# Modulation products in fixed runs of two row blocks, and latent attention with one 96-row tile per head

## The chip, the cores and the metric

The kernel runs on one core of a Trainium2 chip. The time is device microseconds from the start to the end of one execution; less is better. Engines are named PE (TensorE), DVE (VectorE), ACT (ScalarE), POOL (GpSimd) and SP (the engine that issues nearly all DMAs here). All matrices are float32; the dense ones are multiplied in three passes of a rounded type (fp32r, a high and a low part), the small ones plainly in float32, which shows as two records for each matmul.

## What is computed

Two transformer-like blocks on 256 tokens of width 1024: a first block of two layers with modulation by a condition vector (`DEPTH = 2`), and a second of one layer with three mixing branches. Two parts matter here.

The modulation vectors of a layer are a product of two vectors (the condition and its counterpart for the context) with a 1024 x 9216 matrix:

```python
mod_x = (jax.nn.silu(c) @ w_ada[l] + b_ada[l])[:, None, :]
mod_c = jax.nn.silu(c_ctx) @ w_ada[l] + b_ada[l]
```

Latent attention in the second block has 8 heads; each query and key is 64 plain and 32 rotated numbers, the rotated part of the key being shared by all heads:

```python
logits = (jnp.einsum('bhqd,bhkd->bhqk', q_nope[:, :, q0:q1], k_nope[:, :, :q1])
          + jnp.einsum('bhqd,bkd->bhqk', q_rope[:, :, q0:q1], k_rope[:, :q1]))
probs = _masked_softmax(logits * scale, mask)
return jnp.einsum('bhqk,bhkd->bhqd', probs.astype(v.dtype), v[:, :, :q1])
```

The 256 queries go in two blocks of 128; the second sees 256 keys, the first 128.

## The kernel before

**How it is put together.** The Python code doesn't issue instructions. It records them in program order in a `Plan`, with an estimated cost each (`cost`), and `schedule` then lays them out by a list schedule: on each engine, whenever it is free, the earliest recorded operation that is ready and whose buffers find room. `emit` issues the operations in that order, all from line 739, so every row of the profile has that line, and rows are told apart by their forms. Each engine executes its own list in order. A group of matmuls recorded under `with nc.run():` is one operation of the plan: its matmuls stay together, and it has one cost.

**Memory.** SBUF work tiles live in 22 pages of 2048 words per partition (45,056 in all). An operation out of program order gets new buffers only if what in-order execution will need, plus a reserve, still fits (`safe`, `can`); the reserve is the last argument of `schedule` in `build`, `dict(m=4096, s=64)`, and `3000` is how many operations ahead it may go. Some tiles have a cap of their own (`tag`, `bufs`): weights `wraw` 3 landing slots, their high and low halves 4 each, modulation weights `araw` 3 pages.

**Modulation.** `ada_steps(l, g)` makes the steps of group g of layer l: 2048 columns of the matrix in groups 0 to 3, 1024 in group 4. One step per block of 128 rows (eight of them) loads 128 x 2048 words (1 MB) and multiplies it in four products of 512 columns, each with a stationary operand of 32 columns (two vectors, padded), so that product j goes to the array's column strip j and to partitions 32 j of one PSUM bank; half-width groups use two strips. The eight steps add up in the bank, and a last step `fin` turns the result by four products per group into columns. Group 0 of layer 0 is executed at the start, with eight buffers of its own. All others are put in a list (`self.fill`), and one step is taken from it after each gate-and-up step (22) and each down step (16) of a feed-forward block: groups 1 to 4 of layer 0 (36 steps) in the first block, the five groups of layer 1 (45 steps) in the second, and what is left right after the block.

**Latent attention.** `mla_diff` projects queries (`w2_uq`: four 128-column blocks of plain parts, two heads each, then two blocks of rotated parts, four heads each) and keys. `qn`, `kn` hold the plain parts, head h in rows 64 (h % 2) on; `qr` the rotated query parts, head h in rows 32 (h % 4) on; `kr` the rotated key part four times over. `rope32` rotates a 128-row tile. Then for each pair of heads (b) and each head (s): scores of two query blocks, each as a 64-row product and a 32-row product that add up in PSUM; mask, softmax; three transposes; three products with the values, whose outputs go to rows 64 s on. `transposed` and the softmax also serve the branch behind it (differential attention).

The stages by time in the profile: first modulation group to 35 us; feed-forward to 455; mixing to 690; feed-forward to 1115 and, in layer 1, to 1497; mixing to 1648; feed-forward to 1870; then the second block, with the recurrent branch to 2055, latent attention to 2105, differential attention and merging to 2262, feed-forward to the end.

Of the kernel before, what the change touches and what calls it, by code (L numbers as in the profile page):

```python
# [18 lines left out]
P = 128  # L19
# [725 lines left out]
class Build:  # L745
# [134 lines left out]
    def ada_steps(self, l, g):  # L880

        nc = self.nc
        n = min(2048, 9 * D - 2048 * g)
        nj = n // 512
        st = {}

        early = l == 0 and g == 0

        def load(k):
            def f():  # L890
                if k == 0:
                    st["ps"] = self.aux_ps("ada")
                raw = self.sb.tile([P, 2048], F32, name="araw", tag="araw0" if early else "araw",
                                   bufs=8 if early else 3)
                nc.sync.dma_start(raw[:, :n], self.a["w_ada"][l, k, :, 2048 * g:2048 * g + n])
                for j in range(nj):
                    nc.tensor.matmul(st["ps"][32 * j:32 * j + 32, :], self.cs[:, k, :],
                                     raw[:, 512 * j:512 * j + 512], start=(k == 0), stop=(k == KB - 1),
                                     skip_group_check=True, tile_position=(0, 32 * j))
            return f  # L900

        def fin():
            np_ = 32 * nj
            t = self.t("adat", [512])
            nc.vector.tensor_copy(t[:np_], st["ps"][:np_])
            pt = self.aux_ps("adaT")
            for b in range(4):
                nc.tensor.matmul(pt[:, 8 * b:8 * b + 8], t[:np_, 128 * b:128 * b + 128], self.rsel[:np_],
                                 start=True, stop=True)
            view = pt[:, :32].rearrange("p (b j r) -> p b j r", b=4, j=4)[:, :, :nj]  # L910
            dst = self.mod[l][:, 16 * g:16 * g + 4 * nj, :].rearrange("p (j b) r -> p b j r", b=4)
            bia = self.b_ada[l][:, 16 * g:16 * g + 4 * nj, :].rearrange("p (j b) r -> p b j r", b=4)
            nc.vector.tensor_tensor(dst, view, bia, op=OP.add)
            for m in range(2 * g, 2 * g + nj // 2):
                w = self.mod[l][:, KB * m:KB * m + KB, :]
                if m % 3 == 1:
                    i = m // 3
                    nc.vector.scalar_tensor_tensor(
                        self.G[l][i], w, 1.0, self.gains[:, l, i, :, None].to_broadcast([P, KB, 2]),
                        op0=OP.add, op1=OP.mult)  # L920
                elif m in (2, 8):
                    nc.vector.tensor_scalar(self.hg[l][m // 8], w, 0.5, None, op0=OP.mult)
        return [load(k) for k in range(KB)] + [fin]


# [950 lines left out]
    def rope32(self, dst, src):  # L1876
        nc = self.nc
        pr = self.aux_ps("rot")
        nc.tensor.matmul(pr[:, :S], self.perm2, src, start=True, stop=True)
        t1, t2 = self.t256("rp1"), self.t256("rp2")  # L1880
        nc.vector.tensor_tensor(t1, src, self.rope2[:, 0], op=OP.mult)
        nc.vector.tensor_tensor(t2, pr[:, :S], self.rope2[:, 1], op=OP.mult)
        nc.vector.tensor_tensor(dst, t1, t2, op=OP.add)

    def mla_diff(self, u):
# [38 lines left out]
        kr, qr = self.s2("kr", (S,)), self.s2("qr")  # L1924
        self.rope32(kr, x[3])
        qn, kn = ([self.s2(f"{n}{i}") for i in range(2)] for n in ("qn", "kn"))
        w = self.wtile(a["w2_uq"])
        for i in range(3):
# [3 lines left out]
            if i < 2:  # L1932
                nc.scalar.copy(qn[i].rearrange("p a b -> p (a b)"), ps)
            else:
                t = self.t512("qrt")
                nc.scalar.copy(t, ps)
                for j in range(2):
                    self.rope32(qr[:, j], t[:, S * j:S * j + S])
        w = self.wtile(a["w2_ukv"])
        for i in range(2):  # L1940
# [3 lines left out]
            nc.scalar.copy(kn[i].rearrange("p a b -> p (a b)"), ps)  # L1944
# [25 lines left out]
        def transposed(pr):  # L1970
            pt = self.aux_ps("PT2")
            for i in range(3):
                nc.tensor.transpose(pt[:, P * i:P * i + P], pr[:, P * i:P * i + P], self.ident)
# [4 lines left out]
        for b in range(4):  # L1978
            yp = self.aux_ps("y")
            for s in range(2):  # L1980
                h = 2 * b + s
                hs = slice(64 * s, 64 * s + 64)
                rr = slice(32 * (h % 4), 32 * (h % 4) + 32)
                ps = self.aux_ps("Sml")
                for qt, (c0, c1) in enumerate(span):
                    qs = slice(P * qt, P * qt + P)
                    N = c1 - c0
                    nc.tensor.matmul(ps[:, c0:c1], qn[b // 2][hs, b % 2, qs], kn[b // 2][hs, b % 2, :N],
                                     start=True, stop=False)
                    nc.tensor.matmul(ps[:, c0:c1], qr[rr, h // 4, qs], kr[rr, :N], start=False, stop=True,  # L1990
                                     tile_position=(32 * (h % 4), 0))
# [7 lines left out]
                pts = transposed(pr)  # L1999
# [84 lines left out]
def build(tc, aps, out):  # L2084
# [6 lines left out]
    order = plan.schedule(N_PAGES, N_SMALL, W_SLOTS, 3000, dict(m=4096, s=64))  # L2091
# [27 lines left out]
```

## Time and profile before

| | before |
|---|---|
| median of 3 runs (lowest, highest) | 2465.49 us (2462.23, 2465.62) |
| the profiled execution: its time | 2465.52 us |
| its span, first to last instruction | 2463.7 us |
| mean granted TensorE clock | 0.986 |
| TensorE matmul busy | 2419.1 us, 14630 records |
| VectorE busy | 1342.4 us |
| ScalarE busy | 971.2 us |
| GpSimd busy | 46.5 us |
| HBM read | 325.00 MB, 132 GB/s over the span |

Busy time is the union of an engine's instructions; an engine that is busy may still work on a few rows or columns of its array, and successive matmuls overlap in the records by 0.07 to 0.16 us, so sums of durations exceed the time. A clock of 1.00 is 2.4 GHz, 0.50 is 1.2 GHz. In rows by form, `128*32 128x512` is a matmul with 128 rows and 32 columns of stationary operand and 512 columns moving; `page` and `bank` are SBUF and PSUM, `small` the page of small tiles. A window counts every instruction that overlaps it.

### The profile page before, as it was taken

Reading aid. Unit: us, or ns where it says so; the run is one execution under the profiler, and the core shown is the slowest. Engines: PE = TensorE matmul, PEld = TensorE weight load, DVE = VectorE, ACT = ScalarE, POOL = GpSimd, SP = SyncE. Lnnn points to the kernel's source line nnn. Section 1 sums busy time; section 2 is a strip of 40 time slices with the busy share of each in tenths; the row PEclk is TensorE's granted clock in tenths of the full one; section 3 lists DMA queues with packets and bytes.
Section 4 is the critical chain, followed back from the end, with each engine's and each line's share of the span. In section 5 each row is a group of like instructions: output and inputs, shape, how many; then the busy total and the mean of one; then the engine's idle time right before and its main releaser. Section 6 shows DMA issues by size and latency. Waiting matters only on the chain. (4 is left out here: it accounts for less than half of the span.)

```text
span 2463.7 us, 35734 instructions
## 1 busy us (share of the span) xinstructions
PE 2419.1 (98%) x14630; PEld 2036.2 (83%) x14630; DVE 1342.4 (54%) x2533; ACT 971.2 (39%) x1748; POOL 46.5 (2%) x62
## 2 busy tenths in 40 slices
PE   7999999999999999999999999999999999999998
PEld 5777776978787677778878889889999897999998
DVE  4323332585753389335323347866567665657874
ACT  3222222476642122223212235755456122556653
POOL 0000000000000000000000000000000000000000
PEclk8999999999999999999999999999999997999999
DMA  7526523212234454343224223135554011354543
GB/s 312 205 103 240 197 87 127 95 44 87 85 137 161 146 190 180 131 156 139 91 71 137 75 100 103 61 113 178 196 171 164 22 52 35 104 190 169 190 168 123
DMA packets 55043, 328.35 MB, mean 133 GB/s; under 512 B 7134, under 2 KB 10206, under 8 KB 24799
## 3 DMA queue, kind: packets, MB, share of 16 engines
q1 hardware_dynamic: 54878, 326.07, 37.1%
q8 instruction: 114, 1.87, 0.3%
q14 instruction: 51, 0.41, 0.1%
HBM read 325.00 MB, written 1.05 MB: 132 GB/s over the span
## 5 line engine op out<-in xcount | busy, mean ns | idle before, releaser
L739 PE MATMUL bank<-page,page 128*128 128x256 f32 (+8 forms) x13152 | 2296.3, 346 | 29.0 <-DMA page<-in_w_ada_dram 13.2
L739 PEld LDWEIGHTS bank<-page,page 128*128 128x128 f32 (+3 forms) x13152 | 1876.1, 186 | 373.8 <-issue 95.1
L739 ACT CAST page<-w 128x1024 fp32r<-128x1024 f32 (+2 forms) x511 | 489.1, 961 | 1067.6 <-PE bank L739 1027.6
L739 DVE TENSOR_TENSOR page<-w,page 128x1024 fp32r<-128x1024 f32 (+2 forms) x511 | 567.8, 1113 | 591.5 <-ACT page L739 457.8
L739 DVE TENSOR_TENSOR page<-page,bank 128x512 f32<-128x512 f32 (+2 forms) x170 | 94.2, 570 | 245.3 <-PE bank L739 244.1
L739 PE MATMUL bank<-page 128*128 128x256 f32 (+5 forms) x650 | 167.0, 325 | 1.9 <-DVE page L739 1.3
L739 DVE SCALAR_TENSOR_TENSOR page<-bank,small,page 128x256 f32<-128x256 f32 (+2 forms) x240 | 111.5, 484 | 103.8 <-PE bank L739 100.2
L739 DVE TENSOR_TENSOR page<-page,page 128x256 fp32r<-128x256 f32 (+3 forms) x271 | 128.6, 490 | 12.1 <-ACT page L739 11.5
L739 ACT ACTIVATE page<-bank,small 128x256 f32<-128x256 f32 (+2 forms) x216 | 115.1, 546 | 37.3 <-DVE small L739 24.8
L739 PEld LDWEIGHTS bank<-page 128*128 128x128 f32 (+2 forms) x650 | 109.8, 188 | 15.9 <-issue 4.2
L739 ACT CAST page<-page 128x256 fp32r<-128x256 f32 (+1 forms) x167 | 78.2, 481 | 97.0 <-DVE page L739 86.5
L739 ACT COPY page<-bank 128x512 f32<-128x512 f32 (+2 forms) x163 | 77.6, 511 | 96.5 <-PE bank L739 91.1
L739 PEld LDWEIGHTS bank<-small,page 128*128 128x128 f32 (+1 forms) x760 | 93.2, 167 | 25.0 <-issue 8.7
L739 PE MATMUL bank<-small,page 128*128 128x128 f32 (+4 forms) x760 | 108.8, 269 | 4.1 <-ACT page L739 2.8
L739 ACT ACTIVATE page<-bank 128x512 f32<-128x512 f32 (+3 forms) x168 | 84.2, 508 | 61.3 <-PE bank L739 57.8
L739 ACT ACTIVATE page<-page 128x256 f32<-128x256 f32 (+3 forms) x180 | 78.0, 446 | 67.0 <-DVE page L739 60.0
L739 DVE TENSOR_TENSOR page<-bank,page 128x256 f32<-128x256 f32 (+2 forms) x123 | 57.5, 489 | 55.4 <-PE bank L739 29.6
L739 DVE TENSOR_REDUCE small<-bank 128x1 f32<-128x512 f32 (+3 forms) x132 | 67.5, 527 | 4.3 <-PE bank L739 4.0
L739 POOL TENSOR_TENSOR small<-small 128x2 f32<-128x2 f32 (+2 forms) x32 | 34.4, 1078 | 1874.3 <-DVE small L739 1382.8
L739 ACT ACTIVATE page<-page,small 128x256 fp32r<-128x256 f32 (+1 forms) x124 | 56.7, 507 | 30.5 <-DVE page L739 30.0
L739 DVE COPY_PREDICATED page<-page,small 128x384 f32<-128x384 uint32 x124 | 64.9, 590 | 1.0
L739 DVE TENSOR_SCALAR page<-page,small 128x256 f32<-128x256 f32 (+2 forms) x136 | 53.6, 408 | 2.2 <-ACT page L739 1.1
(46 smaller groups left out, 383.2 us busy)
## 6 DMA issues: line engine op xcount, KB each, us to landing
w<-in_gu_dram SPq DMA_DIRECT2D x88, 1024.0 KB, 5.0
page<-in_w_ada_dram SPq DMA_DIRECT2D x64, 1024.0 KB, 4.9
w<-in_dn_dram SPq DMA_DIRECT2D x64, 704.0 KB, 4.1
w<-in_w_up_dram SPq DMA_DIRECT2D x22, 1024.0 KB, 4.8
w<-in_w_qk_dram SPq DMA_DIRECT2D x12, 1024.0 KB, 4.8
w<-in_w_gate_dram SPq DMA_DIRECT2D x12, 1024.0 KB, 4.9
w<-in_w_dn_dram SPq DMA_DIRECT2D x16, 704.0 KB, 4.0
page<-in_w_ada_dram SPq DMA_DIRECT2D x16, 512.0 KB, 3.5
```

The costliest lines, as they stand in the source:

```text
L739: getattr(getattr(self.real, eng), m_)(*a_, **k_)
```

## The change

Modulation: a step now takes two row blocks (`nk = 2`, but one for the early group): two loads, then all their products as one run with a cost of 215 ns a product plus 200. In a half-width group the second block goes to strips 2 and 3, so that these sum separately, and `fin` adds both halves by two products per column block. The buffers `araw` become 4.

Latent attention: `qh`, `kh` hold each head's 64 plain rows and, below them, its 32 rotated rows, in one tile of 96 rows. ScalarE copies each head's 64 rows out of PSUM by itself (`heads`, four copies of 64 x 256 for one of 128 x 512); `rope32` writes the rotated rows head by head; GpSimd copies the rotated key part to all heads. Scores are one product of 96 rows per query block. The transposes are a run; the value products of a pair of heads come together in one run, the two heads by turns.

The reserve of the plan goes from 4096 to 6144 words.

```diff
@@ ada_steps
-        def load(k):
+        nk = 1 if early else 2
+        def load(k0):
             def f():
...
-                raw = self.sb.tile([P, 2048], F32, name="araw", tag="araw0" if early else "araw",
-                                   bufs=8 if early else 3)
-                nc.sync.dma_start(raw[:, :n], self.a["w_ada"][l, k, :, 2048 * g:2048 * g + n])
-                for j in range(nj):
-                    nc.tensor.matmul(st["ps"][32 * j:32 * j + 32, :], self.cs[:, k, :],
-                                     raw[:, 512 * j:512 * j + 512], start=(k == 0), stop=(k == KB - 1),
-                                     skip_group_check=True, tile_position=(0, 32 * j))
+                raws = []
+                for k in range(k0, k0 + nk):
+                    raw = self.sb.tile([P, 2048], F32, name="araw", tag="araw0" if early else "araw",
+                                       bufs=8 if early else 4)
+                    nc.sync.dma_start(raw[:, :n], self.a["w_ada"][l, k, :, 2048 * g:2048 * g + n])
+                    raws.append(raw)
+                with nc.run(cost=nk * nj * 215.0 + 200.0):
+                    for i, raw in enumerate(raws):
+                        k = k0 + i
+                        for j in range(nj):
+                            c = 32 * (j if nj == 4 else j + nj * i)
+                            nc.tensor.matmul(st["ps"][c:c + 32, :], self.cs[:, k, :], raw[:, 512 * j:512 * j + 512],
+                                             start=k < (1 if nj == 4 else 2), stop=k >= KB - (1 if nj == 4 else 2),
+                                             skip_group_check=True, tile_position=(0, c))
...
         def fin():
...
+            m = 2 * nj
             for b in range(4):
-                nc.tensor.matmul(pt[:, 8 * b:8 * b + 8], t[:np_, 128 * b:128 * b + 128], self.rsel[:np_],
-                                 start=True, stop=True)
+                for c in range(0, 8, m):
+                    nc.tensor.matmul(pt[:, 8 * b:8 * b + m], t[:, 128 * b:128 * b + 128], self.rsel[:, c:c + m],
+                                     start=c == 0, stop=c + m == 8)
...
-        return [load(k) for k in range(KB)] + [fin]
+        return [load(k) for k in range(0, KB, nk)] + [fin]
@@ rope32
-        nc.vector.tensor_tensor(dst, t1, t2, op=OP.add)
+        for dst, rows in dsts:
+            nc.vector.tensor_tensor(dst, t1[rows], t2[rows], op=OP.add)
@@ mla_diff
-        qn, kn = ([self.s2(f"{n}{i}") for i in range(2)] for n in ("qn", "kn"))
+        qh, kh = ([self.s2(f"{n}{i}", (4, S)) for i in range(2)] for n in ("qh", "kh"))
+        for i in range(2):
+            nc.gpsimd.tensor_copy(kh[i][64:96], kr[64:96, None, :].to_broadcast([32, 4, S]))
+
+        def heads(dst, i, ps):
+            for j in range(2):
+                for s in range(2):
+                    nc.scalar.copy(dst[i][:64, 2 * j + s], ps[64 * s:64 * s + 64, S * j:S * j + S])
...
-                nc.scalar.copy(qn[i].rearrange("p a b -> p (a b)"), ps)
+                heads(qh, i, ps)
...
-                    self.rope32(qr[:, j], t[:, S * j:S * j + S])
+                    self.rope32([(qh[j][64:96, h], slice(32 * h, 32 * h + 32)) for h in range(4)],
+                                t[:, S * j:S * j + S])
...
-            nc.scalar.copy(kn[i].rearrange("p a b -> p (a b)"), ps)
+            heads(kh, i, ps)
...
         def transposed(pr):
-            for i in range(3):
-                nc.tensor.transpose(pt[:, P * i:P * i + P], pr[:, P * i:P * i + P], self.ident)
+            with nc.run():
+                for i in range(3):
+                    nc.tensor.transpose(pt[:, P * i:P * i + P], pr[:, P * i:P * i + P], self.ident)
...
-                    nc.tensor.matmul(ps[:, c0:c1], qn[b // 2][hs, b % 2, qs], kn[b // 2][hs, b % 2, :N],
-                                     start=True, stop=False)
-                    nc.tensor.matmul(ps[:, c0:c1], qr[rr, h // 4, qs], kr[rr, :N], start=False, stop=True,
-                                     tile_position=(32 * (h % 4), 0))
+                    nc.tensor.matmul(ps[:, c0:c1], qh[h // 4][:96, h % 4, P * qt:P * qt + P],
+                                     kh[h // 4][:96, h % 4, :c1 - c0], start=True, stop=True)
...
+            with nc.run(cost=3 * 215.0):
                 for qt in range(2):
                     for kb in range(qt + 1):
                         c0 = (qt + kb) * P
-                        nc.tensor.matmul(yp[hs, P * qt:P * qt + P], vm[kb][:, 64 * h:64 * h + 64], pts[:, c0:c0 + P],
-                                         start=(kb == 0), stop=(kb == qt), skip_group_check=True)
+                        for s in range(2):
+                            h, hs = 2 * b + s, slice(64 * s, 64 * s + 64)
+                            nc.tensor.matmul(yp[hs, P * qt:P * qt + P], vm[kb][:, 64 * h:64 * h + 64],
+                                             ptss[s][:, c0:c0 + P], start=(kb == 0), stop=(kb == qt),
+                                             skip_group_check=True)
@@ build
-    order = plan.schedule(N_PAGES, N_SMALL, W_SLOTS, 3000, dict(m=4096, s=64))
+    order = plan.schedule(N_PAGES, N_SMALL, W_SLOTS, 3000, dict(m=6144, s=64))
```

## Rows read from the trace of the kernel before

**Rows 1.** The page: busy time, share of the span and instructions of each engine.

```profile
PE 2419.1 (98%) x14630; PEld 2036.2 (83%) x14630; DVE 1342.4 (54%) x2533; ACT 971.2 (39%) x1748; POOL 46.5 (2%) x62
```

**Rows 2.** The page's forty slices: TensorE's granted clock, DMA rate.

```profile
PEclk8999999999999999999999999999999997999999
...
GB/s 312 205 103 240 197 87 127 95 44 87 85 137 161 146 190 180 131 156 139 91 71 137 75 100 103 61 113 178 196 171 164 22 52 35 104 190 169 190 168 123
```

**Rows 3.** Waits of TensorE: us in total, times, longest.

```profile
PE bank L739 <- DMA page<-in_w_ada_dram: 13.2, 5, 6.6
```

**Rows 4.** Groups by form, 35-1200 us: busy us, mean ns, idle.

```profile
L739 PE MATMUL bank<-page,page 128*32 128x512 f32 x512 | 103.5, 604 | 0.0
```

**Rows 5.** By form: stretches at 49.1, 77.9, 693.6 us in turn.

```profile
L739 PE MATMUL bank<-page,page 128*32 128x512 f32 x2 | 1.0, 604 | 0.0
...
L739 PE MATMUL bank<-page,page 128*32 128x512 f32 x8 | 1.1, 604 | 0.0
...
L739 PE MATMUL bank<-page,page 128*32 128x512 f32 x10 | 1.9, 602 | 0.0
```

**Rows 6.** By form: 172-178 us with a load, 132-138 us without.

```profile
L739 PE MATMUL bank<-page,page 128*128 128x512 f32 x23 | 5.7, 395 | 0.0
...
L739 PE MATMUL bank<-page,page 128*128 128x512 f32 x28 | 6.5, 389 | 0.0
```

**Rows 7.** By form, 2055.2-2093.2 us: score products of latent attention.

```profile
L739 PE MATMUL bank<-page,page 32*128 32x256 f32 x16 | 9.2, 673 | 0.0
L739 PE MATMUL bank<-page,page 64*128 64x256 f32 x16 | 8.7, 641 | 0.0
L739 PE MATMUL bank<-page,page 64*128 64x128 f32 x16 | 5.7, 454 | 0.0
L739 PE MATMUL bank<-page,page 32*128 32x128 f32 x16 | 5.7, 452 | 0.0
```

**Rows 8.** By form: 32-row pairs, 2056.5-2057.9 us; last, 2073.1-2075.2 us.

```profile
L739 PE MATMUL bank<-page,page 32*128 32x256 f32 x2 | 0.7, 426 | 0.0
L739 PE MATMUL bank<-page,page 32*128 32x128 f32 x2 | 0.5, 321 | 0.0
...
L739 PE MATMUL bank<-page,page 32*128 32x256 f32 x2 | 1.2, 708 | 0.0
```

**Rows 9.** Stretches: length; busy PE, PEld, DVE, ACT, POOL; TensorE clock; DMA.

```profile
2060.00:2070.00 10.00, 10.00 (x30) 5.75 (x28) 6.55 (x26) 2.13 (x9) 1.05 (x1) 0.60 0.21 89
...
2090.00:2100.00 10.00, 10.00 (x51) 7.64 (x50) 3.09 (x14) 3.92 (x15) 0.00 (x0) 0.69 0.00 0
```

**Rows 10.** By form, 35-1200 us: products that end a modulation group.

```profile
L739 PE MATMUL bank<-small,page 128*128 128x8 f32 x56 | 6.8, 242 | 0.0
```

**Rows 11.** By form, full clock: 256-column products at 2049.9-2050.9 us.

```profile
L739 PE MATMUL bank<-page,page 128*128 128x256 f32 x5 | 1.2, 376 | 0.0
```

**Rows 12.** By form, value-product forms: from 2055.7, 2084.7, 2059.12 us.

```profile
L739 PE MATMUL bank<-page,page 128*64 128x128 f32 x5 | 0.8, 283 | 0.0
...
L739 PE MATMUL bank<-page,page 128*64 128x128 f32 x4 | 1.1, 434 | 0.0
...
L739 PE MATMUL bank<-page,page 128*64 128x128 f32 x4 | 0.4, 298 | 0.0
```

**Rows 13.** By form, whole span: ScalarE copies, GpSimd memsets; last, a weight load.

```profile
L739 ACT COPY page<-bank 128x256 f32<-128x256 f32 x50 | 16.8, 376 | 15.3 <-PE bank L739 14.9
...
L739 POOL MEMSET page<- 64x512 f32 x20 | 10.4, 520 | 449.2 <-PE bank L739 448.5
...
L739 SPq DMA_DIRECT2D w<-in_w_mla_dram x2: 328/328/328, 1895.2 to 1902.4; - x2
```

**Rows 14.** Stretches as in rows 9: a block's edge, the attention stage.

```profile
455.00:470.00 15.00, 13.52 (x96) 12.87 (x95) 12.65 (x30) 7.41 (x17) 2.15 (x2) 0.89 0.30 106
...
2050.00:2140.00 90.00, 88.88 (x475) 67.64 (x474) 41.76 (x114) 34.14 (x81) 1.05 (x1) 0.81 0.22 76
```

**Rows 15.** By form: dense products, 1905-2055 us, then 1505-1645 us.

```profile
L739 PE MATMUL bank<-page,page 128*128 128x256 f32 x258 | 44.5, 301 | 0.0
...
L739 PE MATMUL bank<-page,page 128*128 128x256 f32 x393 | 53.5, 287 | 0.5 <-ACT page L739 0.5
```

More of the change, by code (lines that the diff above doesn't have):

```diff
@@ L887, in ada_steps @@
         early = l == 0 and g == 0
-        def load(k):
+        nk = 1 if early else 2
+        def load(k0):
             def f():
-                if k == 0:
+                if k0 == 0:
                     st["ps"] = self.aux_ps("ada")
-                raw = self.sb.tile([P, 2048], F32, name="araw", tag="araw0" if early else "araw",
-                                   bufs=8 if early else 3)
-                nc.sync.dma_start(raw[:, :n], self.a["w_ada"][l, k, :, 2048 * g:2048 * g + n])
-                for j in range(nj):
-                    nc.tensor.matmul(st["ps"][32 * j:32 * j + 32, :], self.cs[:, k, :],
-                                     raw[:, 512 * j:512 * j + 512], start=(k == 0), stop=(k == KB - 1),
-                                     skip_group_check=True, tile_position=(0, 32 * j))
+                raws = []
[12 more added lines that the diff above has]
+                                             skip_group_check=True, tile_position=(0, c))
@@ L900, in load @@
             return f
         def fin():
-            np_ = 32 * nj
             t = self.t("adat", [512])
-            nc.vector.tensor_copy(t[:np_], st["ps"][:np_])
+            nc.vector.tensor_copy(t, st["ps"])
             pt = self.aux_ps("adaT")
+            m = 2 * nj
             for b in range(4):
-                nc.tensor.matmul(pt[:, 8 * b:8 * b + 8], t[:np_, 128 * b:128 * b + 128], self.rsel[:np_],
-                                 start=True, stop=True)
+                for c in range(0, 8, m):
+                    nc.tensor.matmul(pt[:, 8 * b:8 * b + m], t[:, 128 * b:128 * b + 128], self.rsel[:, c:c + m],
+                                     start=c == 0, stop=c + m == 8)
@@ L1874, in conv_ffn, with rope32 @@
             nc.sync.dma_start(self.out[:, k], t)
-    def rope32(self, dst, src):
+    def rope32(self, dsts, src):
         nc = self.nc
@@ L1923, in mla_diff @@
             cn.append(c)
-        kr, qr = self.s2("kr", (S,)), self.s2("qr")
-        self.rope32(kr, x[3])
-        qn, kn = ([self.s2(f"{n}{i}") for i in range(2)] for n in ("qn", "kn"))
+        kr = self.s2("kr", (S,))
+        self.rope32([(kr, slice(0, P))], x[3])
+        qh, kh = ([self.s2(f"{n}{i}", (4, S)) for i in range(2)] for n in ("qh", "kh"))
[5 more added lines that the diff above has]
+                    nc.scalar.copy(dst[i][:64, 2 * j + s], ps[64 * s:64 * s + 64, S * j:S * j + S])
         w = self.wtile(a["w2_uq"])
@@ L1979, in mla_diff @@
             yp = self.aux_ps("y")
+            ptss = []
             for s in range(2):
                 h = 2 * b + s
-                hs = slice(64 * s, 64 * s + 64)
-                rr = slice(32 * (h % 4), 32 * (h % 4) + 32)
                 ps = self.aux_ps("Sml")
                 for qt, (c0, c1) in enumerate(span):
-                    qs = slice(P * qt, P * qt + P)
-                    N = c1 - c0
-                    nc.tensor.matmul(ps[:, c0:c1], qn[b // 2][hs, b % 2, qs], kn[b // 2][hs, b % 2, :N],
-                                     start=True, stop=False)
-                    nc.tensor.matmul(ps[:, c0:c1], qr[rr, h // 4, qs], kr[rr, :N], start=False, stop=True,
-                                     tile_position=(32 * (h % 4), 0))
+                    nc.tensor.matmul(ps[:, c0:c1], qh[h // 4][:96, h % 4, P * qt:P * qt + P],
+                                     kh[h // 4][:96, h % 4, :c1 - c0], start=True, stop=True)
                 d = diag(ps[:, :3 * P])
@@ L1998, in mla_diff @@
                     nc.vector.tensor_scalar(pr[:, c0:c1], pr[:, c0:c1], st[:, 4 + i:5 + i], None, op0=OP.mult)
-                pts = transposed(pr)
+                ptss.append(transposed(pr))
+            with nc.run(cost=3 * 215.0):
                 for qt in range(2):
```

## The prediction, written before the changed kernel was built

> **What bounds the kernel now.** I read the engines' totals first [rows 1]: TensorE is busy 2419.1 of 2463.7 us (98%), VectorE 54%, ScalarE 39%. Of the 44.6 us in which it is idle, 13.2 are waits for the first modulation weights [rows 3]. So the span is the sum of what TensorE executes, at the clock it is granted, and a busy TensorE is not a full one. So I looked for matmuls that cost more than their columns, by form. Two groups stand out, and both are touched.
>
> The first is the modulation product (form 128*32, 512 columns). A float32 product leaves two records. Away from the start, 512 records keep TensorE busy 103.5 us [rows 4]. The four products of a load go to four column strips: the eight records of such a load end after 1.1 us (1.07 unrounded; second line of [rows 5]), while a single product, two records, takes 1.0 us by itself (first line). So what costs is the stretch, not the product. In order of time the 512 records stand in 94 stretches (38 of eight records, 32 of two, 11 of six, 9 of four, 3 of ten, 1 of twelve), from the one of two records at 49 us [rows 5] to one of four records at 1134.7. Unsplit, 72 loads would be 72 stretches.
>
> The second is latent attention. From 2055 to 2093 us TensorE runs almost nothing but the score products, each as a 64-row and a 32-row product by turns [rows 7]. One 32-row pair of 256 columns takes 0.7 us at 2057 us and 1.2 us at 2074 us [rows 8], and the clock shows why: its mean of 0.60 in 2060 to 2070 us and 0.69 in 2090 to 2100 [rows 9] put it at the lower level, 1.2 GHz, from 2062 to 2096 us, though TensorE is busy in all of it.
>
> **The change part by part.** The sum goes against the profiled execution: span 2463.7 plus 1.8 around it, 2465.5 us, which is the median of the runs (2465.49).
>
> *Modulation runs.* The 56 loads of full groups become 28 runs of two, the 16 half-width loads become 8 runs that fill all four strips. Two loads back to back: the ten-record stretches, which hold four record times in one strip, took 1.9 us [rows 5] (third line). So 28 x 1.9 + 8 x 1.07 = 61.8 us against 103.5: -41.7. At each end of a stretch something more is lost: a window of 6 us with one load has 23 dense products, one without 28 [rows 6]; five of them at 6/26 = 0.23 us (two of the 28 are cut by the edges) are 1.15 us for a stretch of 1.07, so 0.08 us, and 0.3 if a sixth is displaced. I take 0.1 for 94 - 36 = 58 stretches: -5.8. Together -47.5, between -45 and -50. If the second load's strips did not follow without a gap, a run would cost 2 x 1.07: +6. The eight early loads keep their order and wait for their DMA as now: nothing.
>
> Each pair needs two 1 MB transfers landed. They go through SP's queue among the weight loads; a gate-and-up step (48 dense products at 0.23 and a load) lasts 12 us and would move 3 MB, 248 GB/s, less than the 312 GB/s of the first slice [rows 2]. I take nothing; what is queued behind a late one is the next weight tile, whose slots hold a step's worth, and 3.4 us, 1 MB at that rate, is the price each time that cover is gone.
>
> *End of a half-width group.* Four products become eight, in two groups: 16 records more at 6.8/56 = 0.12 us [rows 10], +1.9.
>
> *Scores by one 96-row tile.* The four forms sum to 29.3 us [rows 7]; each of the 32 pairs overlaps the next by some 0.07 us, so 27.1 us of time. The new head has two products, four records, no change of form between. No row has 96 rows. Nearest are the full-height ones: float32 products of 256 columns at 0.215 a record (five in 1.2 us, with a tail of 0.16 [rows 11]), and 0.12 a record for fewer columns [rows 10]. 2 x 0.12 + 2 x 0.215 + 0.1 for entering = 0.77 us a head, 6.2 us for eight. The other end: if a 96-row product pays for its entry like the 32-row ones at the full clock (0.7 us for 256 columns and 0.5 for 128, less two tails of 0.07 [rows 8]), 1.06 us a head, 8.5 us. I take 6.2, since the equal forms in a row of that group [rows 11] pay for entering once: -20.9 (-18.6 at the other end).
>
> *Values, transposes, clock.* The value products of a head are six records: five of this form end after 0.8 us at the full clock, which is when a sixth hands over; four at the lower take 1.1, so six 1.5 [rows 12]. Five heads ran at the first, three at the second: 8.5 us. Taken by turns from two heads they go to two column halves, where four records took 0.4 us [rows 12] (last line): some 0.85 us for a pair of heads, 3.4 for four: -5.1. If they do not run beside each other, 2.8 of it goes. Twelve transposes at the lower clock win 0.13 us each at the full one (half of 1.1/4, the value products' pace), the dense products from 2093 to 2096 us half of 2.9: -1.6 and -1.4. Together -8.1; this and 5.3 us of the score term (first rival) assume the full clock, because the forms whose alternation preceded its fall are gone.
>
> *What is added elsewhere.* Sixteen ScalarE copies of 256 columns at 0.38 us [rows 13] for four of twice the width (under +6 us), six VectorE additions of as many columns more (an estimate at the same price: +2.3), two GpSimd copies of 1024 columns. Those have no row; a 512-column memset took 0.52 us [rows 13], so 1 us each at least and, since they also read, I allow 4, with the group norm's power operations queued behind. ScalarE and VectorE are busy 34 and 42 of 90 us around the stage [rows 14] (second line), so the additions fit. The weights that the rotated key comes from are issued by 1902.3 us [rows 13] (last line), 150 us ahead of the first score product: nothing on the path, up to 3 us without that cover.
>
> *The filler used up sooner.* 45 steps of layer 1 become 25 for 38 places, so none are left for the edge of its feed-forward blocks near 1120 us, where modulation products run now. An edge without them, 455 to 470 us, idles 1.5 us and has 3.3 us at the lower clock, half of them lost [rows 14] (first line): 1.5 + 1.65 = +3.
>
> *The planner's reserve.* 2048 words more of 45,056 are closed to work out of order, the new head tiles take 1536 more, a fourth modulation buffer 2048. Outside the first loads TensorE idles 31 us, so a better order can give back little; a worse one can expose the chains that dense products now cover: in 1905 to 2055 us these are 44.5 us [rows 15]. Bounds -10 to +45; I take +7, near the small end, since in-order work is not touched and a weight tile needs 4096 words, well under what stays open.
>
> Sum: -47.5 + 1.9 - 20.9 - 8.1 + 3 + 7 = -64.6; 2465.5 - 64.6 = 2401 us.
>
> **The rivals.** *The clock stays low in latent attention.* Then each head's scores cost 2 x 0.67 + 0.1 = 1.44 us, 11.5 for 6.2; values 5.9 for 3.4, 24 transposes 0.13 us more each, the dense tail 1.4: +12, 2413 us. For it: the clock fell with TensorE busy, and a quarter of the new stage's TensorE time is transposes. Against: dense products stand in that stage wherever the planner has room. The Trainium skill (TensorE: Matmul & The Clock Gate, Part 4: PE-mode transpose) speaks for this rival: it says that transposes do not count as activity for the clock; no row here isolates them. 0.15.
>
> *Evacuation and softmax become the limit of the stage.* If VectorE's and ScalarE's work of the 90 us [rows 14] ran one after the other, 76 us, only 14 of the 29 us would come back: 2416 us. Against: the two overlap across heads, and the dense projections of the next branch are independent. The Trainium skill (TensorEngine Tiling, PSUM Bottleneck) warns of just this, that tiling speeds up TensorE and leaves the copies out of PSUM as the limit; here VectorE's 42 us fit the 61 that are left. 0.1.
>
> *The reserve starves the run-ahead.* Some of the 44.5 us is exposed: 2415 to 2440 us, centre 2425. 0.14. To end slower than before it must expose over 72 us: all 44.5 around the recurrent branch and half of the 53.5 us of dense records between 1505 and 1645 us [rows 15]; with all of both, 2401 - 7 + 98 = 2492 us. 0.03.
>
> *The change doesn't do what it says*: neither second loads nor head pairs pack: +6 + 2.8, 2410 us. 0.04.
>
> **How the numbers follow.** Forecast 2401 us, 0.54. From 2380 (all gains at their better end, nothing lost to the order) to 2430 holds all but the worst of the reserve. 0.2%, 5 us, is about what a measurement here can tell from no change: faster 0.95, same 0.02, slower 0.03.
>
> **What would show it.** Right: form 128*32 busy some 75 us in all instead of 116, in 36 stretches after the start; no 32-row records; 96-row ones under 7 us; the slice of 2062 to 2094 us without a dip of the clock; TensorE's idle time still under 55 us. Wrong: new waits on ACT or DVE pages between 1900 and 2150 us, or waits on modulation DMA after 35 us; a lower clock with 96-row records in it.

## The result, and the profile of the changed kernel

The changed kernel ("after" below) takes 2391.26 us (median of 4 runs, 2389.5 to 2394.02), the kernel before 2465.55 (2462.23 to 2465.64): a ratio of 0.9703 [0.9686, 0.972], 74.3 us less. The forecast was 2401 us, with a range of 2380 to 2430.

The profiled execution took 2394.02 us (span 2392.2). From its page, the engines' totals and TensorE's granted clock in forty slices:

```profile
PE 2343.3 (98%) x14614; PEld 2024.9 (85%) x14614; DVE 1342.4 (56%) x2539; ACT 973.4 (41%) x1760; POOL 52.2 (2%) x64
...
PEclk8999999999999999999999999999999999999999
```

TensorE is still busy 98% of the span, so the kernel is still the sum of what TensorE executes; this sum fell from 2419.1 us [rows 1] by 75.8. The dip of the clock in the one slice of [rows 2] is gone.

The groups by form of after (engine, operands' shapes, count; busy us, mean ns, idle us): modulation products and the products that end a group, in 35 to 1130 us; one stretch of sixteen records at 60.8 us; the end of the half-width groups (whole span); score products in 2014.74 to 2018.43 us.

```profile
L739 PE MATMUL bank<-page,page 128*32 128x512 f32 x512 | 62.4, 599 | 0.0
L739 PE MATMUL bank<-small,page 128*128 128x8 f32 x56 | 6.8, 241 | 0.0
...
L739 PE MATMUL bank<-page,page 128*32 128x512 f32 x16 | 1.9, 598 | 0.0
...
L739 PE MATMUL bank<-small,page 128*128 128x4 f32 x32 | 3.7, 247 | 0.0
...
L739 PE MATMUL bank<-page,page 96*128 96x256 f32 x12 | 3.6, 385 | 0.0
L739 PE MATMUL bank<-page,page 96*128 96x128 f32 x10 | 1.9, 274 | 0.0
```

The first line answers to [rows 4]: the same 512 records in 62.4 us instead of 103.5. They stand in 36 stretches, 28 of sixteen records and 8 of eight. The last two lines answer to [rows 7]: the second score product of one head and the whole scores of five others fit into these 3.69 us, without a gap. From head to head it is 0.655 us (differences of starts 109, 112, 218 and 216 ns), 5.2 us for eight heads.

Stretches of after (length; busy us and instructions of PE, PEld, DVE, ACT, POOL; TensorE's clock; DMA share; GB/s), an edge of two feed-forward blocks and then latent attention:

```profile
1070.00:1090.00 20.00, 18.32 (x137) 17.66 (x136) 14.70 (x30) 8.60 (x16) 2.96 (x3) 0.91 0.32 106
...
2010.00:2020.00 10.00, 8.96 (x60) 7.28 (x59) 9.04 (x35) 4.92 (x17) 1.11 (x1) 1.00 0.00 0
2020.00:2030.00 10.00, 9.46 (x61) 8.16 (x63) 7.26 (x30) 4.97 (x18) 0.00 (x0) 0.66 0.01 2
2030.00:2040.00 10.00, 10.00 (x97) 9.18 (x92) 7.41 (x19) 8.04 (x21) 0.00 (x0) 1.00 0.51 173
```

Instead of a fall of 34 us with TensorE busy [rows 9] there is one of 6.8 us behind idle time: the eight heads' scores are done so fast that TensorE waits for the first softmaxes (0.83 us at 2019.3, 0.57 at 2020.4, 0.17 at 2021.1).

Waits of TensorE in after (us in total, times, longest), the three largest releasers:

```profile
PE bank L739 <- DMA page<-in_w_ada_dram: 14.0, 5, 7.1
PE bank L739 <- ACT page L739: 11.7, 18, 1.5
PE bank L739 <- DVE page L739: 11.0, 18, 2.3
```

The modulation DMA is waited for five times, as in [rows 3], all in the early group; the paired loads bring no new wait. The softmax does bring one (1.4 us on ScalarE's pages in latent attention), which the prediction had named as a sign of being wrong. All gaps over 0.1 us sum to 42.0 us, against 37.2 before.

### The profile page after: what moved, and what is told of

Read it like the earlier page. It is cut to its first block, busy times and chain, and to the rows that moved or that the text cites. A ratio compares the mean times of both kernels' runs of the same rounds, so it can differ in the third digit from the quotient of the medians.

```text
span 2392.2 us, 35707 instructions
## 1 busy us (share of the span) xinstructions
PE 2343.3 (98%) x14614; PEld 2024.9 (85%) x14614; DVE 1342.4 (56%) x2539; ACT 973.4 (41%) x1760; POOL 52.2 (2%) x64
## 3 DMA queue, kind: packets, MB, share of 16 engines
HBM read 325.00 MB, written 1.05 MB: 136 GB/s over the span
## 5 line engine op out<-in xcount | busy, mean ns | idle before, releaser
L739 PE MATMUL bank<-page,page 128*128 128x256 f32 (+5 forms) x13206 | 2233.9, 344 | 29.6 <-DMA page<-in_w_ada_dram 14.0
L739 PEld LDWEIGHTS bank<-page,page 128*128 128x128 f32 (+2 forms) x13206 | 1875.3, 186 | 318.6 <-issue 61.4
L739 PE MATMUL bank<-page 128*128 128x256 f32 (+9 forms) x564 | 141.1, 315 | 1.7 <-DVE page L739 1.6
L739 PEld LDWEIGHTS bank<-small,page 128*128 128x128 f32 x776 | 95.0, 167 | 25.3 <-ACT page L739 8.1
L739 ACT COPY page<-bank 128x512 f32<-128x512 f32 (+3 forms) x175 | 81.1, 497 | 85.8 <-PE bank L739 84.1
L739 ACT ACTIVATE page<-page 128x256 f32<-128x256 f32 (+3 forms) x180 | 77.9, 446 | 67.1 <-DVE page L739 58.2
L739 PEld LDWEIGHTS bank<-page 128*128 128x128 f32 (+2 forms) x564 | 93.8, 190 | 9.1 <-DVE page L739 2.6
```

Source lines behind the costliest of these rows:

```text
L739: getattr(getattr(self.real, eng), m_)(*a_, **k_)
```

## Experiments

The times of before beside these runs were 2465.3 to 2466.4 us. "Mod" and "Att" stand for the two parts of the change.

### The two parts, each alone, and the reserve

**Mod alone**: the changed kernel with latent attention as before, reserve 6144.

```diff
-        qh, kh = ([self.s2(f"{n}{i}", (4, S)) for i in range(2)] for n in ("qh", "kh"))
+        qn, kn = ([self.s2(f"{n}{i}") for i in range(2)] for n in ("qn", "kn"))
...  (the whole hunks of rope32 and mla_diff taken back)
```

> The kernel before with the modulation part of the change alone (runs of two row blocks, four buffers) and the reserve of 6144 words; latent attention as before. Theory (the prediction's sum, term by term): -47.5 for the runs, +1.9 for the group ends, +3 for the edge without filler, nothing for the reserve: about 2422 us, and the clock still falls in latent attention. Rival (the reserve is what moved the time by giving another order): as much gain as here comes with the kernel before at 6144 alone. Rival (the runs' gain is given back in part by late loads): over 2430 us, with new waits on modulation DMA.

Measured: 2419.33 us (2418.76 to 2420.69), ratio 0.9812 [0.9799, 0.9826], 47.1 us under its before. Latent attention shows the fall of the clock as it was; stretches of this kernel, columns as above:

```profile
2010.00:2020.00 10.00, 10.00 (x46) 6.10 (x44) 6.05 (x20) 2.34 (x9) 1.05 (x1) 0.83 0.30 106
2020.00:2030.00 10.00, 10.00 (x25) 5.72 (x26) 3.31 (x12) 1.86 (x7) 0.00 (x0) 0.50 0.00 0
2030.00:2040.00 10.00, 10.00 (x30) 5.73 (x29) 3.70 (x14) 1.56 (x4) 0.00 (x0) 0.50 0.01 2
2040.00:2050.00 10.00, 10.00 (x33) 7.27 (x34) 4.77 (x23) 3.60 (x14) 0.00 (x0) 0.50 0.00 0
```

**Att alone**, with either reserve: the hunk of `ada_steps` taken back.

```diff
-        nk = 1 if early else 2
...
-        return [load(k) for k in range(0, KB, nk)] + [fin]
+        return [load(k) for k in range(KB)] + [fin]
...  (and, in the second kernel)
-    order = plan.schedule(N_PAGES, N_SMALL, W_SLOTS, 3000, dict(m=6144, s=64))
+    order = plan.schedule(N_PAGES, N_SMALL, W_SLOTS, 3000, dict(m=4096, s=64))
```

With 6144: 

> The kernel before with the latent attention part alone and the reserve of 6144 words; modulation as before. Theory: scores, values, transposes and clock, -29: about 2437 us; form 128*32 still in some 94 stretches. Rival (softmax or evacuation sets the stage's pace): about 2451 us, with waits on ACT and DVE in the stage. If both parts are independent, the two gains of this and of the modulation kernel add up to the whole change's 74 us within 5.

With 4096: 

> The same as the attention kernel, but with the old reserve of 4096 words. Theory (the reserve costs nothing here, the term of +7 was too high): the same time as with 6144 within 4 us. Rival (the larger reserve starves the run-ahead): 7 us or more faster than with 6144. Other rival (the larger reserve gives a better order): 5 us or more slower.

Measured: 2434.77 us (ratio 0.9872 [0.9857, 0.9887]) with 6144, 2437.18 (0.9888 [0.9875, 0.9902]) with 4096. The two intervals overlap. Stretches of latent attention with 6144, then with 4096:

```profile
2060.00:2070.00 10.00, 8.42 (x57) 6.70 (x56) 9.04 (x36) 5.20 (x18) 1.11 (x1) 0.83 0.01 2
```

```profile
2060.00:2070.00 10.00, 8.33 (x61) 6.64 (x60) 9.89 (x44) 6.16 (x23) 1.11 (x1) 1.00 0.00 0
```

TensorE waits for the softmax for 1.6 us in both; the clock falls for 3.4 us in the first and not at all in the second.

**The reserve alone**: before with 6144.

```diff
-    order = plan.schedule(N_PAGES, N_SMALL, W_SLOTS, 3000, dict(m=4096, s=64))
+    order = plan.schedule(N_PAGES, N_SMALL, W_SLOTS, 3000, dict(m=6144, s=64))
```

> The kernel before with the reserve of 6144 words and nothing else changed. Theory: 2465 us within 4. Rival (starved run-ahead): 2472 us or more, TensorE idle by as much more. Rival (the order is what brought the gain): under 2455 us.

Measured: 2461.16 us (11 runs, 2457.54 to 2464.43), 0.9978 [0.997, 0.9987]: 5.3 us less, where the forecast had 7 us more: this larger reserve costs no time here. Its profile, of the fastest of the eleven executions (2457.54 us), has the modulation products in 101.5 us, 2.0 less than [rows 4], by form in 35 to 1200 us:

```profile
L739 PE MATMUL bank<-page,page 128*32 128x512 f32 x512 | 101.5, 604 | 0.0
```

They stand in 92 stretches instead of 94, and the two Att kernels differ in the same way (102.2 us in 92 stretches with 6144, 104.4 in 94 with 4096). So 2 us of the gain are traced. The clock is low in latent attention for 31 us in this execution instead of 34, but for 34 us again in Mod alone, which has the same reserve and the same attention, so this isn't shown to be the reserve's doing; the rest of the gain isn't traced to a place.

Against this kernel, Mod is worth 2461.2 - 2419.3 = 41.8 us and Att 2461.2 - 2434.8 = 26.4. With the 5.3 of the reserve that makes 73.5 of the 74.3: the parts add up. What Mod does with the reserve of 4096 wasn't measured.

### What in the modulation runs gives the gain

Mod alone, but full groups in runs of one row block, with three buffers: the products of a load stay together, yet no two loads are put together in a full group. Half-width groups still pair theirs.

```diff
-        nk = 1 if early else 2
+        nk = 1 if early or n == 2048 else 2
...
-                                       bufs=8 if early else 4)
+                                       bufs=8 if early else 3)
```

> The modulation-only kernel (reserve 6144) with runs of one row block in the full-width groups, three buffers; half-width groups as in the change. It tells what keeping a load's four products together is worth, and what pairing adds. Theory (each stretch pays for entering and leaving): 64 stretches, of 1.07 us each and 0.2 outside, so 28 x (2 x 1.0 - 1.85 + 0.2) = 9.6 us above the paired kernel's 2419: about 2429 us. Rival (the gain is keeping the products together alone, the second block brings nothing): 2419 to 2421. Rival (pairing is most of it): over 2440.

Measured: 2424.0 us (2422.63 to 2425.66), 0.9834 [0.9819, 0.9849]. By form in 35 to 1200 us of this kernel, 62 stretches of eight records and one of sixteen:

```profile
L739 PE MATMUL bank<-page,page 128*32 128x512 f32 x512 | 68.0, 604 | 0.0
```

So 37.2 of the 41.8 us come with this kernel, and 4.7 from pairing the loads of the full groups. Not all of the 37.2 come from keeping the products of one load together, since the half-width groups pair their loads here too. The 32 records of each layer's half-width group, in the kernel with the reserve alone (345 to 430 and 1105 to 1135 us) and then in this one (350 to 395 and 1070 to 1105 us):

```profile
L739 PE MATMUL bank<-page,page 128*32 128x512 f32 x32 | 13.6, 604 | 0.0
...
L739 PE MATMUL bank<-page,page 128*32 128x512 f32 x32 | 9.1, 602 | 0.0
```

```profile
L739 PE MATMUL bank<-page,page 128*32 128x512 f32 x32 | 4.3, 605 | 0.0
...
L739 PE MATMUL bank<-page,page 128*32 128x512 f32 x32 | 4.3, 605 | 0.0
```

They stood in 20 stretches and stand in 8. Each load kept together but unpaired would make 16 stretches of four records, which take 1.05 us each where they occur: 16.8 us instead of 8.6. With 0.2 us at the ends of eight more stretches (worked out below), some 10 of the 37.2 us are pairing as well, and some 27 are keeping a load's products together; this is an estimate from the records, and no run separates the two. Before, each product was a step of its own for the planner, which put other work between them. Pairing takes 68.0 to 62.4 us in the records, and 27 stretch ends go besides: from start to start of the neighbours it is 8.8 us, of which 4.7 show in the time (the intervals of the two kernels, 0.9799 to 0.9826 and 0.9834 to 0.9849, don't overlap); where the rest goes isn't traced.

### What lowers the clock in latent attention

**The 64-row products alone**: before with reserve 6144 and the 32-row products left out.

```diff
                     nc.tensor.matmul(ps[:, c0:c1], qn[b // 2][hs, b % 2, qs], kn[b // 2][hs, b % 2, :N],
-                                     start=True, stop=False)
-                    nc.tensor.matmul(ps[:, c0:c1], qr[rr, h // 4, qs], kr[rr, :N], start=False, stop=True,
-                                     tile_position=(32 * (h % 4), 0))
+                                     start=True, stop=True)
```

> The kernel before with reserve 6144 and without the 32-row score products (the rotated part of the scores is left out of the computation). Scores are then 64-row products only, no alternation of forms within a head. Theory of the prediction (the alternation of forms that drain TensorE let the clock fall): the clock stays at its upper level in latent attention, scores about 6 us, 2437 us. Rival (products with few rows alone do it): the clock falls there again for 10 us or more, scores 11 us, about 2445 us.

**32-row products alone**: before with reserve 6144, the scores of a query block as four equal 32-row products in one strip, so that no two forms of different height alternate.

```diff
-                    nc.tensor.matmul(ps[:, c0:c1], qn[b // 2][hs, b % 2, qs], kn[b // 2][hs, b % 2, :N],
-                                     start=True, stop=False)
-                    nc.tensor.matmul(ps[:, c0:c1], qr[rr, h // 4, qs], kr[rr, :N], start=False, stop=True,
-                                     tile_position=(32 * (h % 4), 0))
+                    for n_ in range(4):
+                        nc.tensor.matmul(ps[:, c0:c1], qr[:32, h // 4, qs], kr[:32, :N], start=n_ == 0, stop=n_ == 3,
+                                         tile_position=(0, 0))
```

> The kernel before with reserve 6144, the scores of latent attention replaced by four 32-row products on one and the same row strip (the computation is changed: only rotated parts, four times over). There is no change of form within or between heads, as few rows as before on the mean, and 8 x 4 x 0.65 = 21 us of products at the full clock. Theory (the alternation of forms let the clock fall for 34 us): no long fall, 2461 - 27 + 21 - 4 = about 2451 us. Rival (products with few rows let it fall, alternation or not): a fall of 20 us or more, scores up to 42 us, about 2470 us.

Measured, one run each: 2436.76 us with 64 rows, which is what the prediction's theory gave (2437), and 2482.97 with 32, which is 13 us above even the rival's 2470. Stretches of the 64-row kernel:

```profile
2060.00:2070.00 10.00, 9.80 (x55) 7.77 (x55) 7.24 (x30) 4.33 (x14) 0.00 (x0) 0.71 0.00 0
2070.00:2080.00 10.00, 10.00 (x84) 8.95 (x83) 6.24 (x20) 7.81 (x22) 0.00 (x0) 1.00 0.01 2
```

and of the 32-row kernel:

```profile
2050.00:2060.00 10.00, 10.00 (x52) 7.96 (x53) 4.26 (x10) 2.53 (x4) 0.00 (x0) 0.79 0.30 106
2060.00:2070.00 10.00, 10.00 (x33) 7.88 (x32) 5.05 (x19) 0.92 (x4) 1.11 (x1) 0.50 0.00 0
...
2100.00:2110.00 10.00, 10.00 (x30) 6.80 (x30) 2.39 (x9) 2.41 (x10) 0.00 (x0) 0.50 0.00 0
2110.00:2120.00 10.00, 10.00 (x48) 8.34 (x47) 2.63 (x9) 1.71 (x7) 0.00 (x0) 0.64 0.01 2
```

TensorE is busy in all of each of these last stretches, and the clock stands at its lower level from 2055.8 to 2117.2 us, 61 us against 34 before, though no scores of two heights alternate. By form in 2062 to 2110 us of this kernel:

```profile
L739 PE MATMUL bank<-page,page 32*128 32x256 f32 x48 | 23.7, 646 | 0.0
L739 PE MATMUL bank<-page,page 32*128 32x128 f32 x48 | 14.2, 443 | 0.0
```

The 32-row products take some 38 of these 48 us. They don't lose time between each other either: within a series they start 427 ns (256 columns) and 213 ns (128 columns) apart at the lower clock, about twice the 216 to 218 and 109 to 112 ns of 96-row products at the full one. So the reason that the prediction gave, the alternation of forms, isn't needed for the fall, and the rival, that work in few rows lowers the clock, holds for 32 rows. Whether an alternation of forms would lower it by itself isn't tested, nor is it traced where the 13 us above the rival's figure go. Without the 32-row products the long fall is absent; the short one left (0.71) begins in 1.1 us of idle time. That kernel's stage is also shorter, so it alone wouldn't have shown it.

**Transposes**: after, with each head's three transposes in latent attention done six times over, 120 more in all.

```diff
-        def transposed(pr):
+        def transposed(pr, times=1):
...
-                for i in range(3):
+                for i in list(range(3)) * times:
...
-                ptss.append(transposed(pr))
+                ptss.append(transposed(pr, 6))
```

> The changed kernel with the three transposes of each head of latent attention done six times over (same result): 120 transposes more in the stage, which are then over half of its small TensorE work. Theory (transposes count like other full-height products, the stage's clock holds): 120 x 0.11 = +13 us, about 2404 us, no long fall of the clock. Rival, by what the Trainium skill (TensorE: Matmul & The Clock Gate, Part 4: PE-mode transpose) states, that transposes do not count as activity: a fall of 15 us or more in the stage, about 2415 to 2430 us.

Measured: 2403.21 us (one run), 12 more than after. By form in 2005 to 2040 us and in 2018.8 to 2025.9 us (where it is the only form), and stretches, of this kernel:

```profile
L739 PE MATMUL bank<-small,page 128*128 128x128 f32 x146 | 17.0, 274 | 1.5 <-ACT page L739 1.5
...
L739 PE MATMUL bank<-small,page 128*128 128x128 f32 x56 | 6.6, 275 | 1.5 <-ACT page L739 1.5
```

```profile
2010.00:2020.00 10.00, 9.16 (x66) 8.04 (x66) 9.07 (x36) 4.26 (x15) 1.11 (x1) 1.00 0.00 0
2020.00:2030.00 10.00, 9.31 (x89) 8.74 (x88) 9.84 (x40) 6.93 (x27) 0.00 (x0) 1.00 0.01 2
2030.00:2040.00 10.00, 10.00 (x103) 9.19 (x102) 1.23 (x4) 2.66 (x6) 0.00 (x0) 1.00 0.31 107
```

Transposes are half of TensorE's time here, and the clock stays full. From 2018.75 to 2025.9 us TensorE executes hardly anything but transposes, with a wait for the softmax of 0.69 us within, and the clock is 1.00 there and behind it. The Trainium skill (TensorE: Matmul & The Clock Gate, Part 4: PE-mode transpose) says that the full clock doesn't engage for transposes, since they don't count as busy in the same way; this one run speaks against that for float32 transposes, as far as keeping a full clock goes.

### The value products of two heads

After, with the value products head by head, as two runs of six records.

```diff
-            with nc.run(cost=3 * 215.0):
+            for s in range(2):
+              with nc.run(cost=3 * 215.0):
...
-                        for s in range(2):
+                        if True:
```

> The changed kernel with the value products of a pair of heads as two runs, one head after the other, instead of by turns. Theory (two column halves work beside each other): 4 x 0.7 = +3 us against the changed kernel, 2394 us, and each run of six records 0.7 to 0.8 us. Rival (they do not overlap): no change.

Measured: 2393.2 us (2392.24 to 2394.11), 0.9708 [0.9691, 0.9724]. That is 1.9 us more than after, as expected in sign, but the intervals overlap: a gain of this part isn't shown. A run of six records by itself takes 0.8 us (at 2023.28 us), as expected. In the records of after, products of the two heads do start 6 to 7 ns apart, so they run beside each other. TensorE waits for the softmax here too (1.7 us), yet its clock doesn't fall (1.00, against 0.66 in after). That isn't the value products' doing as far as the runs go: Att alone with 4096, which has them by turns, shows no fall behind such waits either. The stretch here:

```profile
2020.00:2030.00 10.00, 9.70 (x79) 8.51 (x79) 9.53 (x37) 8.01 (x27) 0.00 (x0) 1.00 0.01 2
```

### Filler at the edges, and a larger reserve

**Edges**: empty places in the list of modulation steps (23 behind group 1 of layer 0, 18 ahead of layer 1), so that the last steps of each layer fall at the edge behind a feed-forward block.

```diff
-            self.fill += self.ada_steps(0, g)
+            self.fill += self.ada_steps(0, g) + [lambda: None] * (23 if g == 1 else 0)
...
+        self.fill += [lambda: None] * 18
```

> The changed kernel with empty places put into the list of modulation steps (23 after group 1 of layer 0, 18 ahead of layer 1), so that the last five steps of each layer fall at the edge behind the feed-forward block. Theory (the +3 us for the edge without filler): both edges lose their idle time of 1.5 us and their fall of the clock: 2391 - 2 x 3 = 2385 us. Rival (the runs delay the chain of the norm by their own length): 2391 or more.

Measured: 2384.68 us (2383.57 to 2386.14), 0.9673 [0.9658, 0.9687], 6.6 us under after and the fastest of all (the intervals touch at 0.9687 and 0.9686; the slowest of its runs is 3.4 us under the fastest of after). The two edges in after, and then in this kernel:

```profile
425.00:450.00 25.00, 23.53 (x184) 23.17 (x183) 16.83 (x35) 11.14 (x22) 2.48 (x2) 0.93 0.26 97
1060.00:1090.00 30.00, 28.32 (x216) 27.51 (x215) 18.37 (x38) 11.12 (x21) 2.96 (x3) 0.94 0.31 105
```

```profile
425.00:450.00 25.00, 24.68 (x187) 19.81 (x187) 16.96 (x43) 10.96 (x23) 1.39 (x2) 0.93 0.43 163
1060.00:1090.00 30.00, 29.69 (x231) 23.81 (x224) 20.07 (x49) 10.83 (x23) 3.99 (x7) 0.94 0.48 176
```

The filler takes away 2.5 us of idle time at the two edges; the short falls of the clock remain there (0.93 and 0.94). The other 4 us aren't traced to the edges: in this profile two short falls around 1604 and 1632 us, worth 3.4 us, are absent, which the filler doesn't touch.

**Reserve 12288** in after.

```diff
-    order = plan.schedule(N_PAGES, N_SMALL, W_SLOTS, 3000, dict(m=6144, s=64))
+    order = plan.schedule(N_PAGES, N_SMALL, W_SLOTS, 3000, dict(m=12288, s=64))
```

> The changed kernel with a reserve of 12288 words instead of 6144: six pages closed to work out of order. Theory of the prediction (a larger reserve exposes chains): 10 us or more slower, over 2400 us, new idle time of TensorE around the recurrent branch. Rival (what stays open is enough, as with 4096 and 6144): within 4 us of 2391.

Measured: 2407.61 us (2405.52 to 2411.28), 0.9763 [0.9746, 0.9779], 16 us more than after. Waits of TensorE in this kernel, 40 to 700 us:

```profile
PE bank L739 <- DMA page<-in_w_ada_dram: 5.3, 4, 2.1
PE bank L739 <- ACT page L739: 3.8, 8, 1.0
PE bank L739 <- DVE page L739: 1.7, 3, 0.9
```

The starving that the prediction feared exists, but begins between 6144 and 12288 words, and its largest new term is late modulation loads: four waits, 5.3 us in all, at 194 to 238 us, in the first feed-forward block (first line; after has none there). The recurrent branch shows no new one. ScalarE is waited for 3.8 us there, against 1.2 in after. Gaps explain 8 of the 16 us (50.1 against 42.0); 3 more are modulation products (78.3 us in the whole span, 75.2 in after), and the rest isn't traced.

## Why the prediction was right, and where it wasn't

**The reading of the bound held.** TensorE's execution time was the sum to work on, and both groups of costly matmuls gave what they cost too much. The forecast was 9.7 us too high; by terms:

**Modulation runs: -47.5 + 1.9 + 3 forecast, -41.8 measured** (Mod against the kernel with the reserve alone), so 0.8 us off. The unit "cost of a stretch" was right: 61.8 us were worked out and 62.4 are there. The price of a stretch's ends was half of what it is: 0.1 us was taken. In the records, the 512-column product ahead of a stretch starts 318 ns before it instead of the usual 227, and the first product behind it loses about as much: 18.7 us for 94 stretches before and 7.4 for 36 after, 0.2 each. It didn't show in the sum, since what the in-stretch busy time counts twice (the overlap with the next product) made up for it: from first start to next start the stretches went from 97.0 to 59.9 us, and 37.1 + 11.3 = 48.4. The Trainium skill (TensorEngine Tiling (Array Packing), Key Properties) says that changing the tiling mode drains TensorE; the 0.2 us agree with that, though no run shows that it is a drain. The group's end costs 3.7 - 2.3 = 1.4 us by form (sixteen 64-row records before were 2.3), near the 1.9.

**The edge without filler: +3 forecast, about +2.8 in the records** (gaps of 1.68 us instead of 0.59, and 3.4 us at the lower clock where there was none). Only the 1.1 us of idle time are tied to the filler. The fall of the clock also stands at this edge in kernels that have their modulation products there: for 3.4 us in Att alone with either reserve and in the 64-row and the 32-row kernels, but not in before or with the reserve alone. The edges kernel gives the idle part back and keeps the fall.

**Scores: 6.2 us forecast, 5.2 measured.** The full-height neighbour [rows 11] was the right one for 96 rows; the 0.1 for entering was paid once for a series, not once per head (the first record behind another form starts its successor after 272 ns, the others after 216 or 218). The line "96-row ones under 7 us" was put carelessly: summed by form they are 4.8 + 3.0 = 7.8 us, because records overlap; without gaps it is 5.2.

**Attention as a whole: -29.0 forecast, -26.4 measured.** The missing 2.6 us have a likely place, though no run shows that it is the cause: in the kernel measured, Att alone with 6144, TensorE waits 1.6 us for the softmax, and 1.7 are lost in 3.4 us at the low clock behind it. The waiting is the second rival, as a small term.

**The clock: right result, wrong reason.** The forecast counted on the full clock "because the forms whose alternation preceded its fall are gone". The 32-row kernel has no such alternation among its scores, and its clock is low for longer. What went with the change was the work in 32 rows. A 96-row tile removes it either way, so the number held by luck; a change that only ordered the forms better would, going by the 32-row kernel, have been predicted wrongly. How many rows are enough isn't shown: the 96-row scores are through within 8.3 us, at the full clock, while in the kernels with 32-row products the fall came 4.6 to 9 us after the first of them, so no run has 96-row products for as long as the fall lasted. The first rival's mechanism, transposes, is refuted as far as the transposes run goes: twice the share it spoke of left the clock full.

**The reserve: +7 forecast, -5.3 measured** on the kernel before (-2.4 with the attention part, where the intervals overlap). This is the step that failed, and 12.3 of the error; modulation and attention, 3.4 the other way, hide part of it. "A better order can give back little" looked only at idle time, and TensorE's idle time didn't fall (46.3 us in the profile with 6144, 44.6 before). But the order also decides how often cheap forms are split, and there busy time is to be had (101.5 for 103.5 us). The other 3 us stay open. The bounds of -10 to +45 did hold it. With 12288 words the feared loss is there, in another place than named.

## To carry over

When TensorE is busy all the time, look for matmuls whose time doesn't follow their columns, and count stretches of a form, not products: keeping the products of one load together was worth some 27 us here, joining two loads some 15 (the split is in part an estimate). Joining two short contractions into one taller tile removes a product and its change of form, and may also remove a fall of the clock that comes with work in few rows. A planner's reserve is not a matter of idle time alone: measure it by itself, since its sign wasn't foreseen here.

## What the runs showed of the hardware

- A TensorE that is busy in every microsecond can stand at 1.2 GHz: for 34 us with 64-row and 32-row products [rows 9], for 61 us mostly with 32-row products in one strip. It didn't with 96-row ones, whose scores last 8.3 us from first to last.
- 144 float32 transposes (two other products share their row), 17.0 of 35 us, left the clock at 1.00, and so did 7 us of hardly anything else.
- Behind like waits for the softmax (1.5 to 1.7 us in all) the clock fell for 6.8 us in after and in the edges kernel, for 3.4 in Att alone with 6144, and not at all in Att alone with 4096, with more transposes or with the value products apart. After, the edges kernel and the two Att kernels share the code of this stage, so the same code can have the fall or not.
- Score products of 64 rows whose heads lie in different row halves start 12 to 14 ns apart in places (64-row kernel, 2051.1 and 2054.1 to 2054.6 us): there they run beside each other without being asked to. From 2054.8 us on, the successive ones start 109 ns or more apart.
- A stretch in column strips costs 0.2 us at its ends on the mean, with short stretches (before) as with long ones (after).
